# First row tile of a batched trace-of-product kernel: one load of 128 partitions against 96 partitions plus four loads of 8

## Chip, cores and metric

One core of one Trainium2 chip. The metric is the device time of one execution in microseconds (us).

## The reference

```python
# a, b: 8 x 2176 x 2176, float32
prod = np.matmul(a, b)
traces = np.diagonal(prod, axis1=1, axis2=2).sum(axis=-1)   # 8 numbers
```

Only the diagonal of each product is needed: the sum over i, j of a[i, j] * b[j, i]. Every element of a and b is used once, so the kernel reads 303 MB and does little with each.

## The kernel before

Rows of `a` come in, TensorE transposes them into `at`, and VectorE multiplies `at` with rows of `b` and sums. Loads of GpSimd convert f32 to bf16 on the way (the page of before has 303.04 MB read from memory and 152.32 MB written by the packets). Only the first row tile of the first `a` is different: SyncE loads it as f32, and ScalarE and VectorE convert it.

```python
stage = ctx.enter_context(tc.tile_pool(name="stage", bufs=3))
# ...
def load(src, start, m, count):          # GpSimd: all other loads, up to 8 blocks of 128 rows
    # ...
    issued = nc.gpsimd.dma_start(out=part, in_=rows)
# ...
def load_first(src, start):              # SyncE: the first tile
    words = stage.tile([P, DOUBLE * ROWS, N], bf16, tag="stage")
    plain = words.bitcast(f32).rearrange("p r k -> p (r k)")[:, :N]
    half = N // 2
    t = single.tile([P, 1, N], bf16, tag="single")
    nc.sync.dma_start(out=plain, in_=src[start:start + P, :])
    nc.scalar.copy(out=t[:, 0, :half], in_=plain[:, :half])
    nc.vector.tensor_copy(out=t[:, 0, half:], in_=plain[:, half:])
    return [(start, 1, t)]
# ...
            if not tiles:
                groups = load_first(a[bi], start)
                ahead, issued = load(a[bi], *loads[1])   # the bulk stream starts beside it
```

At the end VectorE must still work through the last blocks of `b` after they land (from a landing at 699.75 us to 706.95 us in before).

Of the kernel before, what the change touches and what calls it, by code (L numbers as in the profile page):

```python
# [20 lines left out]
def kernel(  # L21
# [6 lines left out]
    nc = tc.nc  # L28
    P = 128
# [12 lines left out]
    a_groups = row_groups(P, even)  # L42
    DOUBLE = 2

    LAST_PIECES = [(0, 2), (2, 3), (3, 5)]

    const = ctx.enter_context(tc.tile_pool(name="const", bufs=1))
# [30 lines left out]
    def load_first(src, start):  # L78

        words = stage.tile([P, DOUBLE * ROWS, N], bf16, tag="stage")  # L80
        plain = words.bitcast(f32).rearrange("p r k -> p (r k)")[:, :N]
        half = N // 2
        t = single.tile([P, 1, N], bf16, tag="single")
        nc.sync.dma_start(out=plain, in_=src[start:start + P, :])
        nc.scalar.copy(out=t[:, 0, :half], in_=plain[:, :half])  # L85
        nc.vector.tensor_copy(out=t[:, 0, half:], in_=plain[:, half:])  # L86
        return [(start, 1, t)]
# [119 lines left out]
    for bi in range(BATCH):  # L207
# [8 lines left out]
        for start, m, count in loads:  # L216
            if not tiles:
                groups = load_first(a[bi], start)
                ahead, issued = load(a[bi], *loads[1])
                with tc.issue_after(issued.ins):  # L220
                    constants()
            elif ahead is not None:
                groups, ahead = ahead, None
            else:
                groups, _ = load(a[bi], start, m, count)
            for start, m, a_t in groups:
                last_transpose = transpose_group(at, a_t, start, m, b_groups)
# [12 lines left out]
        for start, m, count in joined(b_groups):  # L240
            if last and start == N - P:
                v0 = start // P
                b_t = stage.tile([P, DOUBLE * ROWS, N], bf16, tag="stage")
                row = b_t[:, 0, :]
                for g0, g1 in LAST_PIECES:
                    lo, hi = g0 * WIDE, min(g1 * WIDE, N)
# [29 lines left out]
            out=tiles["sums"][:, bi:bi + 1], in_=acc[:, :cols], axis=mybir.AxisListType.X  # L276
# [4 lines left out]
    with tc.issue_after(last_transpose.ins):  # L281
        for n, (x, y) in enumerate(pe_work):
            nc.tensor.matmul(  # L283
                trace_ps, x, y, start=(n == 0), stop=(n == len(pe_work) - 1),
            )
    late_acc = tiles["late"]
    for n, (x, y) in enumerate(late):
# [6 lines left out]
        start=True, stop=True,  # L294
    )
    parts = [tiles["sums"][:, BATCH - 1:BATCH]] + [late_acc[:, n:n + 1] for n in range(len(late) + 1)]
    for n, part in enumerate(parts):
        nc.tensor.matmul(  # L298
            total[:, BATCH - 1:BATCH], tiles["ones"], part,
            start=(n == 0), stop=(n == len(parts) - 1),  # L300
# [3 lines left out]
        out=out.rearrange("(a b) -> a b", a=1),  # L304
        in_=tiles["result"][:1, :BATCH],
# [31 lines left out]
```

## Time and profile before

| | before |
|---|---|
| median of the first runs | 711.2 us (711.15 to 711.58) |
| span of the profiled run | 709.4 us |
| first tile lands | 5.67 us |
| last load of two blocks lands | 699.75 us |

The prediction below reads the page, the stretches and the chain of waits of this run.

### The profile page before, as it was taken

To read this page: it belongs to the slowest core of one execution; us is meant where nothing else is said; L and a number is where in the kernel's file an instruction comes from. 1 tells how busy PE (TensorE), PEld (TensorE's weight loads), DVE (VectorE), ACT (ScalarE), POOL (GpSimd) and SP (SyncE) were. 2 spreads that over 40 slices of the span, in tenths; PEclk is the share of its full clock that TensorE was granted. 3 is DMA by queue.
4 is the path that set the end of the run, shared out by engine and by line. 5 is a ranking of instruction groups with operands and counts; after the bars stand their busy time and mean duration, and the time that the engine had idled before them with its cause. 6 is when DMAs were issued, how large, how long until landed. Compare 5 with 4: busy or idle time off the path is not lost.

```text
span 709.4 us, 3709 instructions
## 1 busy us (share of the span) xinstructions
PE 206.3 (29%) x1406; PEld 193.0 (27%) x1406; DVE 411.4 (58%) x449; ACT 196.8 (28%) x210; POOL 34.6 (5%) x60
## 2 busy tenths in 40 slices
PE   1542005420065100542006510065100560005655
PEld 0542005410065100541005510065000550005655
DVE  0223996139952399514994259932599335993356
ACT  2443005430064200633006420065200651006610
POOL 1000000000010000100000000000000000000000
PEclk9977557765577655766557665577655775557776
DMA  9999999999999999999999999999999999999996
GB/s 220 220 220 219 206 219 220 219 217 209 219 220 218 217 212 216 220 219 215 212 218 220 218 213 215 215 222 217 215 214 213 225 217 212 215 217 222 219 207 138
DMA packets 11620, 152.32 MB, mean 215 GB/s; under 512 B 850, under 2 KB 1106, under 8 KB 3282
## 3 DMA queue, kind: packets, MB, share of 16 engines
q0 software_dynamic: 11456, 150.97, 100.1%
q1 hardware_dynamic: 146, 1.11, 0.4%
q8 instruction: 11, 0.18, 0.1%
q14 instruction: 7, 0.06, 0.0%
HBM read 303.04 MB, written 0.00 MB: 427 GB/s over the span
## 4 chain that ended last, share of the span: by engine, by line
DMA 56%; DVE 34%; issue 7%; PE 2%; another core or an unknown queue 2%; POOL 0%; DVEq 0%; POOLq 0%
DMA t<-in_b_dram 43%; DVE scratch L122 33%; DMA t<-in_a_dram 13%; PE ps L155 1%; DVE acc L122 0%; DVEq L122 0%; PE ps L176 0%; POOL identity masks.py:199 0%; DVE at L110 0%; POOL identity masks.py:197 0%; PE total L298 0%; DVE result L302 0%; DVE late L122 0%; POOLq L74 0%
## 5 line engine op out<-in xcount | busy, mean ns | idle before, releaser
L122 DVE CUSTOM_DVE_ANT_1 scratch<-at,t 128x2048 bf16<-128x2048 bf16 (+1 forms) x156 | 310.6, 1991 | 74.9 <-DMA t<-in_b_dram 67.7
L112 ACT COPY at<-ps 128x1024 bf16<-128x1024 bf16 x208 | 194.4, 1044 | 474.9 <-PE ps L155 474.5
L155 PE MATMUL ps<-identity,t 128*128 128x128 f32 x1071 | 177.9, 334 | 482.5 <-DVE sums L275 262.7
L155 PEld LDWEIGHTS ps<-identity,t 128*128 128x128 f32 x1071 | 166.2, 213 | 490.8 <-DVE sums L275 311.2
L110 DVE COPY at<-ps 128x1024 bf16<-128x1024 bf16 (+2 forms) x104 | 93.5, 902 | 214.4 <-PE ps L155 196.9
L74 POOL DMA_DIRECT2D t<-in_a_dram x23 | 15.3, 663 | 354.3 <-PE ps L176 156.5
L74 POOL DMA_DIRECT2D t<-in_b_dram x26 | 16.8, 645 | 288.3 <-PE ps L176 147.5
L283 PEld LDWEIGHTS <-at 128*128 128x128 bf16 x153 | 17.1, 122 | 13.3 <-issue 12.7
L283 PE MATMUL trace_ps<-t,at 128*128 128x128 bf16 x144 | 16.7, 293 | 12.3 <-DMA t<-in_b_dram 12.3
L176 PE MATMUL ps<-identity,t 128*128 128x128 bf16 x170 | 16.4, 219 | 4.9 <-DVE at L110 4.8
L176 PEld LDWEIGHTS <-t 128*128 128x128 bf16 x170 | 13.0, 100 | 8.3 <-issue 8.0
L122 DVE DVE_READ_ACCUMULATOR2_ANT acc<- 128x1 f32 x163 | 13.3, 81 | 0.0
L86 DVE CAST t<-words 128x1088 bf16<-128x1088 f32 x1 | 0.7, 726 | 4.8 <-DMA words<-in_a_dram 4.8
L247 POOL DMA_DIRECT2D b_t<-in_b_dram x3 | 1.6, 537 | 16.0 <-DVE acc L122 16.0
L122 DVE CUSTOM_DVE_ANT_0 scratch<-at,t 128x128 bf16<-128x128 bf16 x7 | 2.0, 291 | 0.2
L85 ACT CAST t<-words 128x1088 bf16<-128x1088 f32 x1 | 1.1, 1099 | 3.7 <-DMA words<-in_a_dram 3.7
L122 DVE CUSTOM_DVE_ANT_1 scratch<-at,b_t 128x256 bf16<-128x256 bf16 (+1 forms) x3 | 1.5, 510 | 0.1
L275 DVE TENSOR_REDUCE sums<-acc 128x1 f32<-128x22 f32 (+1 forms) x8 | 1.4, 174 | 0.3
L85 ACT ACT_TABLE_LOAD x1 | 1.3, 1283 | 0.7 <-PEq L321 0.7
L283 PE MATMUL trace_ps<-b_t,at 128*128 128x128 bf16 x9 | 1.3, 284 | 0.4 <-DMA b_t<-in_b_dram 0.4
L298 PE MATMUL total<-late,ones 128*1 128x1 f32 x8 | 0.8, 164 | 0.8 <-DVE late L122 0.8
L298 PEld LDWEIGHTS total<-late,ones 128*1 128x1 f32 x8 | 0.3, 80 | 1.2 <-DVE late L122 1.2
(14 smaller groups left out, 2.7 us busy)
## 6 DMA issues: line engine op xcount, KB each, us to landing
t<-in_a_dram POOLq DMA_DIRECT2D x16, 4352.0 KB, 46.7
t<-in_b_dram POOLq DMA_DIRECT2D x15, 4352.0 KB, 51.5
t<-in_b_dram POOLq DMA_DIRECT2D x9, 544.0 KB, 54.5
t<-in_a_dram POOLq DMA_DIRECT2D x7, 544.0 KB, 53.0
t<-in_b_dram POOLq DMA_DIRECT2D x1, 2176.0 KB, 42.9
words<-in_a_dram SPq DMA_DIRECT2D x1, 1088.0 KB, 4.9
t<-in_b_dram POOLq DMA_DIRECT2D x1, 1088.0 KB, 25.7
b_t<-in_b_dram POOLq DMA_DIRECT2D x1, 256.0 KB, 11.7
```

The costliest lines, as they stand in the source:

```text
L74: issued = nc.gpsimd.dma_start(out=part, in_=rows)
L85: nc.scalar.copy(out=t[:, 0, :half], in_=plain[:, :half])
L86: nc.vector.tensor_copy(out=t[:, 0, half:], in_=plain[:, half:])
L110: last_copy = nc.vector.tensor_copy(out=dst, in_=src)
L112: nc.scalar.copy(out=dst, in_=src)
L122: nc.vector.tensor_tensor_reduce(out=out, in0=x, in1=y, scale=1.0, scalar=0.0, op0=MUL, op1=ADD, accum_out=acc,)
L155: nc.tensor.transpose(ps[:, n * m + r, :], words[:, r, c0:c0 + step * (P - 1) + 1:step], tiles[f32],)
L176: last_transpose = nc.tensor.transpose(ps16[:, n, r, :], a_t[:, r, c0:c0 + P], tiles[bf16],)
L247: nc.gpsimd.dma_start(out=row[:, lo:hi], in_=b[bi, start:start + P, lo:hi])
L275: nc.vector.reduce_sum(out=tiles["sums"][:, bi:bi + 1], in_=acc[:, :cols], axis=mybir.AxisListType.X)
L283: nc.tensor.matmul(trace_ps, x, y, start=(n == 0), stop=(n == len(pe_work) - 1),)
L298: nc.tensor.matmul(total[:, BATCH - 1:BATCH], tiles["ones"], part, start=(n == 0), stop=(n == len(parts) - 1),)
```

## The change

The intent, by its form and its description: give eight of the 16 DMA engines four rows of their own on top of 6 for all, and so move a quarter of the other eight engines' rows to them (10 rows and 6 rows in place of 8 and 8). The trace of before doesn't show how a load of 8 rows is dealt. The step of 4 keeps the partitions of a small load apart.

```diff
+    FIRST_SPLIT = [(32, P, 1), (0, 32, 4), (1, 32, 4), (2, 32, 4), (3, 32, 4)]
...
-        nc.sync.dma_start(out=plain, in_=src[start:start + P, :])
+        for lo, hi, step in FIRST_SPLIT:
+            nc.sync.dma_start(
+                out=plain[lo:hi:step, :], in_=src[start + lo:start + hi:step, :]
+            )
```

## The prediction

The count from which the sum starts: 6 rows for each of 16 engines from the load of 96, and one more for each of eight engines from each load of 8 rows. This was the assumption. So the eight "low" engines get 10 rows and the eight "high" ones 6, where before had 8 each; low, lowest and high, here and in the expectations, only tell these groups apart, since the traces carry no engine numbers. From 2 rows at the measured 0.325 us come the 0.65 us more and less, and the sum came to +0.3 us: 711.2 + 0.3 = 711.5 us. The 1.28 us of a turn is the distance of bulk packets on an engine in before; that a small load waits for one of them was an assumption as well.

> **What bounds the kernel now.** I read the page first (busy shares, the 40 slices, the queues), then the groups, the stretches of the run, the chain of waits, and last the completion records of the transfers themselves.
>
> The page, span and slices:
>
> ```profile
> span 709.4 us, 3709 instructions
> ...
> DMA  9999999999999999999999999999999999999996
> ...
> q0 software_dynamic: 11456, 150.97, 100.1%
> q1 hardware_dynamic: 146, 1.11, 0.4%
> ...
> HBM read 303.04 MB, written 0.00 MB: 427 GB/s over the span
> ```
>
> The 16 DMA engines have work in every slice but the last. The busiest compute engine, VectorE, is busy for 58% of the span (411.4 us). Nearly everything goes through the queue that GpSimd feeds (q0); the load that the change touches is the only one on q1 apart from the 32-byte result.
>
> The stretches of the run (columns: stretch, its length, busy us of each engine, granted clock, DMA share, GB/s):
>
> ```profile
> 2.00:5.00 3.00, 0.00 (x0) 0.00 (x0) 0.00 (x0) 0.02 (x1) 1.64 (x6) 1.00 0.89 351
> 5.00:20.00 15.00, 2.06 (x9) 1.72 (x9) 0.95 (x2) 3.02 (x3) 0.71 (x1) 1.00 1.04 221
> 20.00:46.00 26.00, 10.93 (x72) 10.55 (x72) 5.69 (x6) 11.28 (x12) 1.28 (x2) 0.92 1.00 214
> 46.00:680.00 634.00, 174.67 (x1162) 163.21 (x1163) 384.05 (x412) 181.22 (x194) 28.47 (x44) 0.62 1.02 217
> 680.00:697.00 17.00, 12.44 (x108) 12.14 (x108) 13.80 (x12) 0.00 (x0) 1.59 (x3) 0.70 1.02 214
> ```
>
> From 5 us on the share is 1.00 or above: a transfer always follows a transfer. (The GB/s are bytes written; those loads write bf16 for the f32 that they read, hence about half of the 427.)
>
> The start, from the timeline:
>
> ```profile
> 0.74 0.40 SPq L84 DMA_DIRECT2D words<-in_a_dram  x1
> ...
> 1.25 0.82 POOL L74 DMA_DIRECT2D t<-in_a_dram  x1 [0.80 <-POOLq L321]
> ...
> 5.70 1.10 ACT L85 CAST t<-words 128x1088 bf16<-128x1088 f32 x1 [3.68 <-DMA words<-in_a_dram]
> 5.70 0.73 DVE L86 CAST t<-words 128x1088 bf16<-128x1088 f32 x1 [4.83 <-DMA words<-in_a_dram]
> ...
> 7.09 0.71 POOL L74 DMA_DIRECT2D t<-in_b_dram  x1 [3.45 <-ACT t L85]
> ...
> 26.31 3.72 PEld L155 LDWEIGHTS ps<-identity,t 128*128 128x128 f32 x18 [17.68 <-DMA t<-in_a_dram]
> ```
>
> The reader should see the slack. The first tile is cast at 5.7 us, but when that work is over TensorE waits 17.68 us for the next load. GpSimd's third issue, at 7.09 us, waits for the cast to free the buffer; the two loads already queued keep the DMA busy until about 46 us (the second lands at 46.84 us).
>
> The end, from the chain of waits:
>
> ```profile
> 674.06 25.69 DMA t<-in_b_dram
> 699.75 0.03 issue
> ```
>
> VectorE starts the last 2-block load's product 0.16 us after it lands at 699.75 us, and from there its instructions follow almost back to back to 706.95 us. So the end is that landing plus a fixed tail of about 9.6 us (709.4 - 699.75), and the landing is that of the slowest of 16 engines.
>
> That slowest engine is the point of this case. Each GpSimd load leaves 16 completion records in the trace, one per DMA engine, without its number. Their spread, from the first to the last of one load, in ns (my sums from the trace):
>
> ```
> load landing near 25.8 us: 461      46.4: 455      66.9: 1578
> 154.4: 1511   218.7: 1526   460.4: 1842   635.3: 2352   658.5: 2639
> the load at 697.1, all sixteen: 0 151 271 304 494 571 | 1191 1202 1371 1377 1435 1446 1548 | 2261 2386 2634
> ```
>
> The engines run one packet after another, never idle, and drift apart only by steps. Ten steps of about 1.1 us each follow the ten 16 KB instruction packets that lie inside the stream (the page's q8 line has eleven); each hit another engine until the ninth and tenth hit the engines of the first and second. So eight engines take these packets in turn. Smaller steps of 0.3 to 0.55 us go with the 8 KB packets of q14; the engine at 2386 collected four of those and none of the big ones.
>
> [...] 128 packets of 8,704 B and 16 completion packets on q1. [...]
>
> [...]
>
> [...] In the trace the 16 KB packets do get in amid a bulk load (one at 51.6 us, inside the load of 46.4 to 66.9)[...]. Yet no q0 packet starts before an engine has finished its q1 share, so how SyncE's packets and GpSimd's mix is open.
>
> [...]
>
> **The change, part by part.** Removed: one load of 128 rows, 8 rows per engine. In the trace a row takes 0.325 us per engine in steady state (packets 0.328 us long, 3 to 4 ns overlapped), and the engines finish their share between 4.89 and 5.36 us.
>
> [...] Against before: 2 x 0.325 = 0.65 us more on each low engine, 0.65 us less on each high one. The total stays the same, 128 rows.
>
> Issue cost: five issues at 0.40 us from 0.74 us on end at about 2.75 us; the low engines work on their first six rows until about 4.2 us (5.0 - 2 x 0.325, with some spread), so the small loads should be there in time. Landing of the tile: 5.67 + 0.65 = 6.3 us without mixing. If a bulk packet takes a turn before each small load, 4 x 1.28 = 5.1 us are added: 11.4 us.
>
> Moved: in the built program ScalarE's table load (1.28 us) now waits for the four small loads, so its cast starts 1.3 us after landing, at 7.6 to 12.7 us. GpSimd's third issue follows at 9 to 14 us. Both are hidden: the next load arrives at 26.3 us, and the queue is full until 46 us. SyncE has nothing else to do. Instruction counts on the other engines stay the same, and the race check passes.
>
> On the path: only the shift between engines. As they are never idle after the first load, +0.65 and -0.65 us ride on to the end. With the sixteen offsets above:
> - the slowest engine (2634) is a low one: its new offset is 3284, the end is 0.65 us later;
> - it is high and the 2386 one is low: 2386 + 650 = 3036, +0.40 us; if only the 2261 one is low, 2911, +0.28 us;
> - all three are high: the slowest becomes at most 1548 + 650 = 2198, -0.44 us.
>
> Which engines are low the trace doesn't tell. By its form the change is meant to relieve the high eight, so I lean to those being the eight that take instruction packets. But then the 2386 engine, not one of them, is low and becomes the last: up to +0.40 us, less if the new start order gives it a better place than the 0.47 us that it began with. Hence 0.0 to +0.4 in the likelier half, +0.28 to +0.65 in most of the rest, -0.44 in a small part. I take +0.3: 711.2 + 0.3 = 711.5 us.
>
> **Rivals.** (1) The balance works: the late engines are all high, and 0.4 us or a little more is won: 710.7 us. For it: the whole shape of the change. Against: two unrelated causes of delay fell on disjoint engines. (2) The small loads wait whole bulk loads for their turn, not single packets: one load is 20.5 us per engine, two are queued, so the tile lands near 47 us. Then the DMA runs dry for some 3 us until the third issue brings data: 714 us. [...] (3) The first tile now sits on the path, and its later landing delays all: at most 6 us, but the 17.68 us idle says that it is hidden; 711.2 us. [...]
>
> **Range and chances.** Runs of before lie within 0.43 us, and the shift cannot exceed 0.65 us by itself. 710.6 to 712.3 us should hold the time 8 times in 10; the rest is for rival 2, another chip, or fetches that fall elsewhere. Two per cent would be 14 us, which nothing here can move: faster 0.005, same 0.985, slower 0.01.
>
> **What would show it.** In the profile after: five issues on SyncE; engines leaving q1 in two groups, eight near 4.3 us and eight near 5.6 us or later; TensorE's wait for the second load still ended by that load at 26 to 27 us; DMA slices still 9; the spread of a load at 25 to 46 us near 1.7 us in place of 0.46; in the last loads a spread above 2.63 us if a low engine is last, below if the change balances. Wrong would be: a DMA slice under 9 near 46 us (rival 2), no two groups (then 96 rows or 8 rows are not split as I assumed), or a time outside the range with the DMA still full, which would mean that the rate itself changed.

## More of the kernel before

Where a run has "rounds", it was timed in turn with the kernel before on the same chip.

The columns are the stretch in us, its length, busy us of PE, weight loads, VectorE, ScalarE and GpSimd with the number of instructions, the granted clock, the DMA share and GB/s written. These are the stretches while the first tile is loaded:

```profile
3.00:3.80 0.80, 0.00 (x0) 0.00 (x0) 0.00 (x0) 0.00 (x0) 0.65 (x1) 1.00 1.00 424
3.80:4.80 1.00, 0.00 (x0) 0.00 (x0) 0.00 (x0) 0.00 (x0) 0.00 (x0) 1.00 1.01 426
```

The load from SyncE moves 424 to 426 GB/s with all engines busy; this is f32 to f32, so bytes written equal bytes read.

## The result, and the profile after

712.6 us (712.56 to 712.71, 4 runs) against 711.17 us of before (711.01 to 711.58, 4 runs). The ratio is 1.0019, 95% interval 1.0002 to 1.0037. By the 2% rule this is the same; by the records it is 1.4 us slower. Ratios are the mean time of one kernel's runs over that of the other's of the same rounds, so not quite the ratio of the medians. The forecast of 711.5 us, with 710.6 to 712.3 us, was too low.

The page after:

```profile
span 710.8 us, 3721 instructions
...
DMA  9999999999999999999999999999999999999996
...
q0 software_dynamic: 11456, 150.97, 99.8%
q1 hardware_dynamic: 178, 1.11, 0.6%
...
HBM read 303.04 MB, written 0.00 MB: 426 GB/s over the span
```

The same bytes, the same full slices. The q1 queue has 178 packets, 32 more than before: the rows are 128 again, but 16 + 4 x 8 = 48 completion packets stand in place of 16. This agrees with eight engines for a load of 8 rows.

The stretches after:

```profile
2.00:5.00 3.00, 0.00 (x0) 0.00 (x0) 0.00 (x0) 0.00 (x0) 1.64 (x6) 1.00 0.90 258
5.00:20.00 15.00, 0.98 (x5) 1.01 (x6) 0.73 (x1) 2.38 (x2) 0.71 (x1) 1.00 1.04 228
20.00:46.00 26.00, 11.54 (x78) 10.62 (x76) 5.93 (x7) 13.11 (x14) 1.28 (x2) 0.92 1.00 214
46.00:680.00 634.00, 172.29 (x1162) 160.38 (x1163) 384.14 (x412) 180.92 (x194) 28.47 (x44) 0.63 1.02 217
```

From 20 us on nothing differs. The loss is in the first stretch: 258 GB/s where before had 351, at the same DMA share (0.90 and 0.89). A busy share doesn't tell how fast a transfer goes; the GB/s beside it do. Narrower stretches after:

```profile
3.00:3.80 0.80, 0.00 (x0) 0.00 (x0) 0.00 (x0) 0.00 (x0) 0.65 (x1) 1.00 1.10 359
3.80:4.80 1.00, 0.00 (x0) 0.00 (x0) 0.00 (x0) 0.00 (x0) 0.00 (x0) 1.00 0.99 252
```

252 in place of 426 GB/s with every engine busy. In the packets behind it (my sums from the trace), a row that starts between 3.8 and 4.8 us takes 0.51 to 0.57 us; before it took 0.33 us. No bulk packet starts before 4.9 us in either kernel, so this is not the bulk stream taking turns.

The start after, from the timeline:

```profile
0.75 3.22 SPq L88 DMA_DIRECT2D words<-in_a_dram  x5
...
16.48 1.28 ACT L91 ACT_TABLE_LOAD   x1 [16.48 <-DMA words<-in_a_dram]
16.51 0.73 DVE L92 CAST t<-words 128x1088 bf16<-128x1088 f32 x1 [15.64 <-DMA words<-in_a_dram]
17.77 1.10 ACT L91 CAST t<-words 128x1088 bf16<-128x1088 f32 x1
...
19.17 0.71 POOL L77 DMA_DIRECT2D t<-in_b_dram  x1 [15.52 <-ACT t L91]
...
28.00 2.22 PEld L161 LDWEIGHTS ps<-identity,t 128*128 128x128 f32 x11 [7.29 <-DMA t<-in_a_dram]
```

The tile is cast from 16.5 us on, not 5.7 us, and GpSimd's third issue moved from 7.1 to 19.2 us. But TensorE still waits 7.29 us for the second load, as it waited 17.68 us before. All this is in the shade.

The chain of waits after, its start and its end:

```profile
3.35 13.04 DMA words<-in_a_dram
...
19.17 49.90 DMA t<-in_b_dram
```

```profile
675.04 26.11 DMA t<-in_b_dram
701.16 0.03 issue
```

The first of these is a trap: the chain now leads through the first tile, because the third load was issued by the cast that waited for it. But that load took 49.90 us to land since it stood in a queue, and an earlier issue would only have stood longer: issued 12.1 us earlier in before, it had its last completion packet at 68.19 us, here at 68.72 us. The second pair carries the time: the load of two blocks lands at 701.15 us (675.04 + 26.11), 1.40 us later than at 699.75 us, and the rest of the 1.43 us follows.

Which engine is last? Every load leaves a 4-byte completion packet per engine on q0, and its place behind the first one is stable to some ns from load to load, so an engine can be followed by its place (my tracking from the trace; places in ns):

```
first bulk load, before, 25.464 us + 0 54 117 157 283 302 303 308 308 326 348 349 384 437 452 502
first bulk load, after,  25.445 us + 0 82 273 395 399 442 453 895 | 1321 1449 1551 1641 1711 1911 1989 2136
engine with four 8 KB packets, before:  253 -> 784 -> 1314 -> 1845 -> 2375
engine with four 8 KB packets, after:  1989 -> 2520 -> 3050 -> 3581 -> 4111
last engine before (two 16 KB packets): 439 -> 1559 -> 2686
```

After, there are two groups of eight, as forecast. The mean of the first eight is 0.06 us later than the mean of all sixteen before, and the mean of the other eight 1.41 us later. The engine of the four 8 KB packets is in the late group and ends last. That it stood at 253 ns before, and not at the 489 ns of another engine, follows from its packets: a bulk packet starts every 1.285 us on an engine, and the one before its first 8 KB packet ends at 108.03 us, 14.0 such steps after the completion at 253 ns and 13.8 after the one at 489 ns. Each of its four steps is then 0.53 us. It can also be followed without places, since the bulk packet behind each of these four takes 1.51 us: the fourth 8 KB packet starts at 627.84 us before and at 629.53 us after, 1.69 us later.

### The profile page after: what moved, and what is told of

It is laid out like the page before. It is cut to its first block, busy times and chain, and to the rows that moved or that the text cites. A ratio compares the mean times of both kernels' runs of the same rounds, so it can differ in the third digit from the quotient of the medians.

```text
span 710.8 us, 3721 instructions
## 1 busy us (share of the span) xinstructions
PE 203.2 (29%) x1406; PEld 189.3 (27%) x1406; DVE 411.5 (58%) x449; ACT 196.4 (28%) x210; POOL 34.6 (5%) x60
## 4 chain that ended last, share of the span: by engine, by line
DMA 58%; DVE 34%; issue 7%; SPq 0%; ACT 0%; DVEq 0%; another core or an unknown queue 0%; PE 0%; POOLq 0%; ACTq 0%
DMA t<-in_b_dram 50%; DVE scratch L128 33%; DMA t<-in_a_dram 7%; DMA words<-in_a_dram 2%; DVE acc L128 0%; SPq L88 0%; ACT L91 0%; ACT t L91 0%; DVEq L128 0%; PE total L304 0%; DVE result L308 0%; DVE late L128 0%; POOLq L77 0%; DVE sums L281 0%
## 5 line engine op out<-in xcount | busy, mean ns | idle before, releaser
L161 PE MATMUL ps<-identity,t 128*128 128x128 f32 x1071 | 174.9, 328 | 485.8 <-DMA t<-in_a_dram 254.9
L161 PEld LDWEIGHTS ps<-identity,t 128*128 128x128 f32 x1071 | 162.6, 212 | 495.0 <-DVE sums L281 366.2
L289 PE MATMUL trace_ps<-t,at 128*128 128x128 bf16 x144 | 16.5, 291 | 12.8 <-DMA t<-in_b_dram 12.8
L182 PE MATMUL ps<-identity,t 128*128 128x128 bf16 x170 | 16.4, 219 | 5.4 <-DVE at L116 5.1
L91 ACT ACT_TABLE_LOAD x1 | 1.3, 1283 | 16.5 <-DMA words<-in_a_dram 16.5
L253 POOL DMA_DIRECT2D b_t<-in_b_dram x3 | 1.6, 537 | 16.4 <-DVE acc L128 16.4
```

Source lines behind the costliest of these rows:

```text
L161: nc.tensor.transpose(ps[:, n * m + r, :], words[:, r, c0:c0 + step * (P - 1) + 1:step], tiles[f32],)
L182: last_transpose = nc.tensor.transpose(ps16[:, n, r, :], a_t[:, r, c0:c0 + P], tiles[bf16],)
L253: nc.gpsimd.dma_start(out=row[:, lo:hi], in_=b[bi, start:start + P, lo:hi])
L289: nc.tensor.matmul(trace_ps, x, y, start=(n == 0), stop=(n == len(pe_work) - 1),)
```

## The experiments

All runs but the two marked wrong gave the right result. For each I give the median time, the 0.8 or 1.0 us stretch of the page that shows the rate, and the landing of the load of two blocks from the chain of waits (before 699.75, after 701.15 us). The time intervals of the ratios are about 0.0013 wide on each side, so gains of half a microsecond rest on the traces, not on the times alone. The landing is that of the one execution that was profiled; its time is within 0.2 us of the median, but for e5_no_step (713.63 us).

| run | time, us | before in its rounds | ratio (95%) | slowest landing, us |
|---|---|---|---|---|
| e1_96_32 | 712.28 | 711.19 | 1.0016 (1.0003 to 1.0028) | 700.81 |
| e2_full_plus2 | 711.64 | 711.19 | 1.0006 (0.9993 to 1.0020) | 700.41 |
| e3_halves | 712.04 | 711.19 | 1.0012 (0.9999 to 1.0024) | 700.56 |
| e4_halves_step2 | 711.46 | 711.19 | 1.0004 (0.9991 to 1.0016) | 699.95 |
| e5_no_step | 713.20 | 711.15 | 1.0031 (1.0019 to 1.0044) | 702.26 |
| e6_all_ports | 712.02 | 711.15 | 1.0013 (1.0000 to 1.0025) | 700.69 |
| e7_full_plus4 | 712.26 | 711.15 | 1.0017 (1.0004 to 1.0029) | 701.01 |
| e8_four_plus2 | 711.58 | 711.15 | 1.0007 (0.9993 to 1.0021) | 700.14 |
| e9_mem_contig | 712.46 | 711.10 | 1.0017 (1.0003 to 1.0030) | 701.11 |
| e10_ports_half | 712.18 | 711.10 | 1.0016 (1.0002 to 1.0030) | 700.64 |
| e11_again | 712.32 | 711.10 | 1.0019 (1.0005 to 1.0032) | 700.93 |

The theory after the result (A): the loss has two parts. The imbalance does what was forecast, plus or minus 0.65 us; and the 96-row load is slow for all engines, because of the partitions that it writes. The rivals: the small loads slow the rows (B), the imbalance alone makes the loss (C), the place of the rows in memory is what slows (D). "Ports" stands for a guess within A: that rows written to some sets of partitions slow each other. No run shows why; what the runs show is which loads were slow. The 0.65 us for a row is twice the measured 0.325 us, the 1.3 us in e5_no_step four times: estimates. Rows per engine are counts of the plan.

**e1_96_32**: the 96 rows kept, the rest balanced.

```diff
-    FIRST_SPLIT = [(32, P, 1), (0, 32, 4), (1, 32, 4), (2, 32, 4), (3, 32, 4)]
+    FIRST_SPLIT = [(32, P, 1), (0, 32, 1)]
```

> The 96 rows stay, the other 32 go in one load over 16 engines, 2 rows each: every engine carries 8 rows, as before the change, so the imbalance is gone and only the form of the 96-row load stays. Theory A (the 96-row load itself slows its rows, from 0.33 to about 0.55 us[...]): rows of the first load are again about 0.55 us from the fourth on, the engines start the bulk stream 0.5 us or more later than before the change, all alike (spread under 1 us, no two groups of eight), and the end is 0.5 to 1.0 us later than before: 711.7 to 712.2 us. Theory B (the small loads, by their issues or descriptors, slow the rows): rows at 0.33 us, end as before, 711.2 us. Theory C (imbalance alone makes the loss): as B.

712.28 us. The stretches:

```profile
3.00:3.80 0.80, 0.00 (x0) 0.00 (x0) 0.00 (x0) 0.00 (x0) 0.66 (x1) 1.00 1.17 370
3.80:4.80 1.00, 0.00 (x0) 0.00 (x0) 0.00 (x0) 0.00 (x0) 0.00 (x0) 1.00 1.01 261
```

261 GB/s without any small load, and no two groups: the mean of the sixteen places is 1.03 us later than before. So the 96-row load is slow by itself, and neither B nor C is the whole cause. The time is a little above the stated range, since the load of 32 rows is slow as well (rows of 0.58 to 0.68 us).

**e2_full_plus2**: the full load kept, only the imbalance added.

```diff
-        for lo, hi, step in FIRST_SPLIT: ...
+        nc.sync.dma_start(out=plain, in_=src[start:start + P, :])      # as FIRST_SPLIT = [(0, P, 1)]
+        spare = words.bitcast(f32).rearrange("p r k -> p (r k)")[:, N:2 * N]
+        for lo in range(2):
+            nc.sync.dma_start(out=spare[lo:32:4, :], in_=src[start + lo:start + 32:4, :])
```

> The full 128-row load, as before the change, plus two loads of 8 rows (step 4) into unused space: the pure imbalance of the change, 2 rows more on each low engine, with no 96-row load. All engines: rows at 0.33 us if theory A holds[...], near 0.5 us if theory B holds (small loads slow the rows). Low eight: bulk stream begins 0.65 to 0.70 us later than before, high eight as before (0 us). The last engine of the changed kernel is a low one that is hit by four 8 KB packets; before the change it was 0.25 us ahead of the last, so 0.68 - 0.25 = 0.43 us later at the end, up to 0.65 us if its first place is worse: 711.6 to 711.9 us. The result must still be right.

711.64 us, in the range. The landing is 0.66 us later. The rows stay fast:

```profile
3.80:4.80 1.00, 0.00 (x0) 0.00 (x0) 0.00 (x0) 0.00 (x0) 0.00 (x0) 1.00 1.04 435
```

So small loads don't slow the rows (B falls), and the landing is about as late as expected, 0.43 to 0.65 us. But the engine named there is not the last. Its fourth 8 KB packet starts at 628.56 us, 0.72 us later than before, and it ends 0.19 us ahead of another engine of the late group, which got two 16 KB packets.

**e7_full_plus4**: the same with `range(4)`.

> The full load of before plus four loads of 8 rows into unused space: 4 rows more on each low engine, the high ones as before. If a row on the low engines rides on to the end unchanged: 2 more rows than the run with two such loads, so 0.65 to 0.7 us more than that run at the slowest landing near the end, 1.3 us later than before in all: 712.2 to 712.6 us. If the engines even out along the way, as much as the run with two loads, 711.6 us.

712.26 us, 0.62 us above e2; the landing 0.60 us later than in e2. Two rows more on the low engines ride on to the end. On the engine with four 8 KB packets nothing is lost: its fourth one starts at 629.27 us, 1.43 us later than before and 0.71 us later than in e2, or 0.36 us for each small load of a row and its completion. The landing shows less, since another engine was last in e2. The engines don't even out in 700 us.

**e8_four_plus2**: two loads of 4 rows (`lo:16:4`) in place of two of 8.

> The full load of before plus two loads of 4 rows[...]: four engines start the bulk stream 0.65 to 0.7 us late, twelve as before. If the engine that is last at the end is among the lowest 4: 0.45 to 0.65 us later as with 8 engines, 711.6 to 711.8 us. If it is not: at most 0.3 us later, 711.2 to 711.4 us.

711.58 us, and the landing 0.39 us later. Four engines begin late (places 816 to 1144 ns, the other twelve up to 496), so a load of 4 rows does use four engines. The time fell between the two cases, but the trace settles it: the engine with four 8 KB packets is one of the four (its fourth such packet starts at 628.49 us, 0.65 us later than before), and followed by its places it is the last. So this run is the forecast's sum without the 96-row load: 0.65 us more on an engine that was 0.25 us ahead of the last, +0.40 us, against 0.39 us at the landing.

**e3_halves** and **e4_halves_step2**: two loads of 64 rows, by the plan 4 per engine and no imbalance; contiguous halves, or even and odd rows.

```diff
-    FIRST_SPLIT = [(32, P, 1), (0, 32, 4), (1, 32, 4), (2, 32, 4), (3, 32, 4)]
+    FIRST_SPLIT = [(64, P, 1), (0, 64, 1)]      # e3_halves
+    FIRST_SPLIT = [(0, P, 2), (1, P, 2)]        # e4_halves_step2
```

> Two loads of 64 contiguous rows, 64 to 127 and then 0 to 63, 4 rows per engine each, no small loads and no imbalance. [...] Theory A (ports): [...]rows take near 0.65 us nearly throughout, 8 rows end about 2 us later than before (near 7 us), and the end is 1 to 2.5 us later, 712.2 to 713.7 us, the same on all engines. Theory B or a loss by more issues only: rows at 0.33 us, 711.2 us.

> Two loads of 64 rows again, but the even and then the odd rows: [...]per engine 4 rows each as in the contiguous halves. Theory A in its plain form[...]: rows at 0.33 us, end as before, 711.2 us. [...] Theory D (reading other places of memory at once is what slows, not the ports): no clear difference from the contiguous halves.

712.04 us and 711.46 us. The stretch of the contiguous halves, then that of the even and odd rows:

```profile
3.00:3.80 0.80, 0.00 (x0) 0.00 (x0) 0.00 (x0) 0.00 (x0) 0.65 (x1) 1.00 1.12 272
```

```profile
3.00:3.80 0.80, 0.00 (x0) 0.00 (x0) 0.00 (x0) 0.00 (x0) 0.65 (x1) 1.00 0.97 403
```

272 against 403 GB/s; rows that start from 3.5 to 4.0 us take 0.69 us (median) in the first and 0.33 us in the second. A row of the contiguous halves takes twice the time, as A expected. But these two differ in the place in memory as well (D). The time of e3 is below the range: its second half goes between bulk packets, where a row takes 0.34 us again, so only the first half pays. And e4 is 0.27 us late with fast rows; its 64th row is done at 4.25 us, that of before at 3.96 us. Its first row starts at 2.03 us, that of before at 1.77 us. So it does in every run here whose first load has 64 rows (2.05 to 2.10 us in e3, e6, e9 and e10), whatever partitions it writes; why is open.

**e9_mem_contig** and **e10_ports_half**: partitions written and rows read taken apart. Both give a wrong result, since rows land on other partitions.

```diff
+        for h in range(2):   # e9_mem_contig: contiguous in memory, every second partition
+            nc.sync.dma_start(out=plain[h:P:2, :], in_=src[start + 64 * h:start + 64 * (h + 1), :])
+        for h in range(2):   # e10_ports_half: every second row of memory, contiguous partitions
+            nc.sync.dma_start(out=plain[64 * h:64 * (h + 1), :], in_=src[start + h:start + P:2, :])
```

> Wrong result on purpose (the rows of the first tile land on other partitions). Two loads of 64 rows: each reads 64 contiguous rows of memory and writes every second partition[...]. If the ports slow the contiguous halves: rows at 0.33 us, some 400 GB/s or more between 3.8 and 4.8 us, time near that of the even and odd rows, 711.3 to 711.6 us. If the place of the rows in memory does: rows near 0.65 us, under 300 GB/s per busy engine set, 711.9 us or more.

> Wrong result on purpose, the opposite: each load reads every second row of memory and writes 64 contiguous partitions[...]. If ports: rows near 0.65 us, under 300 GB/s between 3 and 3.8 us, time near that of the contiguous halves, 711.8 to 712.3 us. If memory: rows at 0.33 us, 711.3 to 711.6 us.

The stretch of e9_mem_contig, then of e10_ports_half:

```profile
3.00:3.80 0.80, 0.00 (x0) 0.00 (x0) 0.00 (x0) 0.00 (x0) 0.65 (x1) 1.00 1.58 490
```

```profile
3.00:3.80 0.80, 0.00 (x0) 0.00 (x0) 0.00 (x0) 0.00 (x0) 0.65 (x1) 1.00 1.08 283
```

Rows take 0.33 us in e9 and 0.68 us in e10 (median of those that start from 3.5 to 4.0 us). The partitions written decide, not the rows read: D falls. (The 490 GB/s has a share of 1.58, as bulk packets already overlap there; the row durations are the cleaner reading.)

The time of e10, 712.18 us, is as stated. That of e9, 712.46 us, is not: it is a miss by 0.9 us. Three of its four executions took 712.45 to 712.54 us, and one 711.60 us, as stated. In the profiled one, of 712.54 us, fifteen of its engines start the bulk stream well (places 0 to 669 ns), but one at 1555 ns; this one also gets two 16 KB packets and is last by 1.3 us at the landing of two blocks. In e3, e6 and e9 one of the first bulk packets was recorded with 2.3, 2.3 and 2.1 us where 1.3 is usual, and one engine is behind its fellows from there. What holds up that packet is open; the execution of 711.60 us suggests that it doesn't happen every time, but no trace of that one was kept.

**e6_all_ports**: the imbalance of the change, 10 and 6 rows, in loads that write every second or every fourth partition.

```diff
+    FIRST_SPLIT = [(0, P, 2), (1, P, 4), (3, 32, 4), (35, 64, 4), (67, 96, 4), (99, P, 4)]
```

> The imbalance of the change (10 rows on each low engine, 6 on each high one) without its 96-row load: 64 even rows, then 32 rows in steps of 4, then four loads of 8 rows in steps of 4[...]. If the common loss of 0.7 us in the changed kernel came from the crowded 96-row load: rows at 0.33 us, high engines about 0.5 us earlier and low ones about 0.7 to 0.9 us later than before the change, two groups of eight, and the end 0.5 to 0.9 us later than before: 711.7 to 712.1 us, half of the change's loss. If more and smaller loads cost something of their own, the end is as late as the change's, 712.6 us or more.

712.02 us, 0.87 us later than before and 0.6 us better than the change's 712.6: in the range. The median row takes 0.33 to 0.34 us from 3 us on. But the agreement is partly luck. The early eight start only 0.15 us earlier than before, not 0.5; the 64th row is done at 4.60 us (before 3.96), which may be why. And one engine of the late group starts 0.9 us behind the next. So the run bounds what such steps can win back; it doesn't isolate the imbalance as e2 and e7 do.

Its timeline shows how much a late first tile is worth:

```profile
24.69 0.71 POOL L77 DMA_DIRECT2D t<-in_b_dram  x1 [21.04 <-ACT t L91]
...
28.37 1.79 PEld L161 LDWEIGHTS ps<-identity,t 128*128 128x128 f32 x9 [2.15 <-DMA t<-in_a_dram]
```

The third issue comes at 24.69 us and TensorE still waits 2.15 us for the second load. The queue lasts until 46 us, so even this lateness is hidden.

**e5_no_step**: the step of 4 taken out of the small loads.

```diff
-    FIRST_SPLIT = [(32, P, 1), (0, 32, 4), (1, 32, 4), (2, 32, 4), (3, 32, 4)]
+    FIRST_SPLIT = [(32, P, 1), (0, 8, 1), (8, 16, 1), (16, 24, 1), (24, 32, 1)]
```

> The change without its step: the four small loads take rows 0 to 7, 8 to 15, 16 to 23, 24 to 31[...]. If the step does what it is meant for[...], a small row takes from 0.34 us up to 1.3 us, and the low engines lose up to 4 us more: 713 to 716 us. If the bulk packets between them hold the small rows of different engines apart in time, or the crowding of a few rows is short, the time stays that of the change, 712.6 us with 0.3 us either way.

713.2 us, 0.6 us above the change: the lower edge of the first case. The second of the four small rows is slow, 0.83 to 0.93 us on the eight engines; in the change it takes 0.34 us. The first takes about 0.6 us in both, while rows of the 96-row load still run, and the third and fourth 0.34 us. Also the first bulk packets of nearly all engines now take 1.5 to 1.9 us in place of 1.3. So the step is worth having here, and the cost without it is partly borne by the bulk packets that run at the same time.

**e11_again**: the changed kernel once more, on the chip of e9 and e10.

> The changed kernel again on this chip. If the order of the engines follows from the program: the end is again 1.3 to 1.6 us later than before, the first load's completions again fall into two groups of eight with 0.3 us or more between them, the slowest engine again one of the late group with four 8 KB packets. If it is chance of one execution, another engine is last and the time differs by some tenths of a us.

712.32 us, 1.2 us later than before in its rounds; a little less than stated. Two groups again (0 to 911 ns and 1143 to 1644 ns), with only 0.23 us between them. At the landing of two blocks two engines are last within 0.01 us of each other, both of the late group: the one of the four 8 KB packets, and one that got two 16 KB packets. The places within a group change from execution to execution by some tenths; the groups and the loss stay.

No version here beats the kernel before. The arithmetic says why: before, the last engines were one of the early group (2686 ns by the tracking) and two of the late group (2375 and 2255 ns). Which group an engine is in is read off the changed kernel, by the instruction packets that hit it, taking it that they go to the same engines in both. Moving rows either way between the two groups helps one of these and hurts another.

That they go to the same engines is not safe for every run. In before, after and e2 the first three 16 KB packets take about 962, 893 and 893 ns, but in e1, e3, e5 and e9 about 949, 945 and 936 ns, and the 962 ns come later in the same order: they seem to begin at another engine there. In e7 both engines that get two of them are late ones, in e5 both are early ones. So part of the differences of some tenths between the landings of these runs can come from the engine that these packets began with, and no run controls that.

## Why the prediction was wrong

**Right.** The kernel is bound by DMA (a share of 1.00 to 1.04 from 5 to 697 us, before and after), and only the place of the slowest engine moved. The hidden parts stayed hidden: the later cast, the table load that waits, the third issue. The imbalance has about the forecast size: the two groups differ by 1.35 us in their means (1.09 us in e11), against 1.30 us forecast (2 x 0.65), and e8 confirms the sum of +0.40 us. The engine named as last, the one at 2386 ns with four 8 KB packets, was low and did become the last, though in e11 only in a tie. Rival 1, that the balance works, failed for the reason given. Rivals 2 and 3 did not happen.

**The step that failed** is "0.65 us more on each low engine, 0.65 us less on each high one". It took 0.325 us a row, measured on a load of 128 rows, for a load of 96. Measured was 1.41 us more and 0.06 us more. Both are about 0.7 us above the forecast: the 96th row of the first tile was done at 5.36 us in place of 4.62 us, 0.74 us later, at median rows of 0.37 to 0.56 us. The forecast had a slow 96-row load among its rivals as (4), for a reason that no run shows, but held it to cost the high engines only and to matter only in rival 1. It costs all sixteen, since the 96-row load runs at 252 GB/s as a whole. The last of the prediction's own signs of being wrong is the one that came: a time outside the range with the DMA still full, "which would mean that the rate itself changed".

The sum for the engine that ended last:

| term | forecast | measured |
|---|---|---|
| its distance from the last engine, before | -0.25 | -0.31 (2375 less 2686 ns by the packets; -0.25 by the landing records) |
| two more rows | +0.65 | +0.72 (its fourth 8 KB packet, e2 less before) |
| slow 96-row load | 0 | +0.97 (the same packet, after less e2) |
| sum | +0.40 | +1.38; the landing moved by 1.40 |

The 0.97 is this engine's own. Its group's mean moved by 1.41 us, 0.69 us more than the two rows; the other 0.28 us is a late place within the group (1989 ns, where the mean is 1714 ns). The headline number had been lowered from +0.40 to +0.3 in the hope of a better place in the start order than "the 0.47 us that it began with". That was a misreading: the engine began at 0.25 us, near the mean of all sixteen (0.29 us), and it got a worse place, not a better one. The range reached to +1.1 us only.

**Mis-sized, without harm:** the issues and the tile's landing. The five issues were to end at 2.75 us; they took 3.22 us in all and ended at 3.97 us, still before the low engines had done their first six rows. For the landing the forecast had 6.3 us, or 11.4 us if a bulk packet takes a turn before each small load; it landed at 16.4 us. In the packets, a low engine does its six rows and one small row, each with its completion, without a bulk packet between; then one bulk packet goes ahead of each of the three other rows (on seven of the eight engines two ahead of the first of these), and one more ahead of each row's completion, so seven of them at 1.28 us.

**Open:** why a first load of 64 rows starts its rows 0.3 us later (e3, e4, e6, e9, e10), what holds up one engine's first bulk packet (e3, e6, e9), how exactly 96 rows are dealt to the engines, and which partitions slow each other and by what; and which engine the instruction packets begin with. That the partitions written are the cause is shown for 64 rows (rows of 0.33 us in e9 against 0.68 us in e10); for 96 rows it is carried over by the same signature, full share at about 0.6 of the rate (252 against 426 GB/s).

## What to carry to other kernels

Here all DMA engines stayed busy nearly to the end (a share of 1.00 or above from 5 us on to 697 us), and a transfer's position hardly mattered (a first tile that landed at 16.4 us in place of 5.7 us was in the shade), but its cost on the slowest engine did: four extra rows on an engine still cost it 1.43 us some 600 us later (e7). Before splitting a 128-partition load into parts, measure the rows of each part: a part of 64 contiguous partitions took twice as long for each row as one of every second partition (0.69 us in e3 against 0.33 in e4) with every engine "busy", so read the GB/s, not the share. And before balancing engines, find which ones are late for which reason; here two kinds of instruction packets (16 KB, about 1.1 us each, and 8 KB, 0.53 us each) made late engines in both groups, so shifting rows between the groups could not win.
